# Queries of two cross-attention heads as one 2x2x2 block product in seven

## The chip, the cores and the metric

The kernel runs on one core of one Trainium2 chip. The metric is device microseconds (us) of one execution; a time is the median of several executions. Durations of single instructions and waits come from one further execution, which was taken with the hardware profiler.

## The reference

One layer of a streaming encoder on 512 tokens of width 1024, in float32:

```python
h = x + concat(A, B) @ W_out          # A: forgetting attention, B: gated recurrence
hn = rmsnorm(h, norm_x_g)
q = (hn @ w_q).reshape(b, s, 4, 256)  # 1024 x 1024 weights, four heads of 256 columns
k, v = split(rmsnorm(mem, norm_mem_g) @ w_kv)          # 256 memory tokens
p = softmax(q k^T / sqrt(256)); o = p v
h = h + o.reshape(b, s, 1024) @ w_o
h = h + square(relu(rmsnorm(h) @ w1)) @ w2             # d_ff = 4096
return rmsnorm(h)
```

The change concerns `hn @ w_q`, and in it heads 2 and 3: a product of 512 output columns, 512 tokens and an inner size of 1024.

## The kernel before

**Products.** Every float32 operand is kept as two tiles, `hi` (rounded to the matmul's type) and `lo` (what is missing), and each product is three matmuls: hi·hi, lo·hi and hi·lo (`gemm_fm`, L316 to L318). A weight panel of 1024 x 256 comes by DMA as two raw halves of 128 partitions x 1024 elements (`wr30a`, `wr30b`). Of each, ACT makes the hi part (L184, `wh...`), and DVE the lo part (L188, `wl...`). The split tiles live in four buffers, so the split of a panel half waits until the matmuls that read the half four places earlier are done. A panel's split is issued when an earlier panel is taken up by `next_panel`, and a scheduler gives it its place in the engine's order.

**Order.** Each engine runs its instructions in the order in which the program has them. A `fill` object holds generators of matmul groups (a "step" is the group for one or more slices of the inner size); `fill.run(x)` puts about x us of steps at this place of TensorE's order, and `fill.until(name)` all steps up to a named one.

**Cross attention.** After `residual(..., "wo", ...)`, which adds the output projection to the stream chunk by chunk (DVE L1317 `hT`, ACT L1318 `x1_hi`, DVE L1319 `x1_lo`), head 0's queries are projected (`x_proj(0)`), and the four heads then run one after the other. Per head and half of the tokens (`tp` 0 and 1): `x_scores` makes 12 matmuls of 256 columns (L1377 to L1379, `xs`), the row maximum on DVE (L1381, `xm`), its scaled negative (L1383, `xn`), two exponentials on ACT (L1388), a reciprocal (L1389) and two scalings on DVE (L1391, `xp`). `x_T_` transposes the probabilities on TensorE (L1400, `xpt`), ACT and DVE split them (L1451 `pth`, L1452 `ptl`), and `x_out` multiplies by the values (L1408 to L1410, `xo`) and writes `o_hi` (ACT, L1411) and `o_lo` (DVE, L1412). The scale of the softmax, `r16`, comes out of the mean square `pm1` by a short chain on GpSimd (L437, L440, L1368).

While a head's softmax runs on DVE and ACT, TensorE does filling work between the steps:

- in head 0, head 1's queries (`x_proj(1)`, tiles `xq10`, `xq11`);
- in heads 1 and 2, the queries of heads 2 and 3 (`x_proj(2)`, `x_proj(3)`: four tiles of 24 matmuls of 512 columns);
- in head 3, the first six of eight slices of three output chunks `xw0`, `xw1`, `xw2` of the next projection (`early` in `residual`); the rest follows `x_out(3)`.

**Sums of weights.** The feed-forward part that follows already uses products in seven. A weight sum for them is a copy of a block into DRAM (issued by SyncE, the list `copies`) and an accumulating DMA (issued by GpSimd, `Presum`), which are let go one by one at a pace given in us of TensorE work, `PACE`.

Of the kernel before, what the change touches and what calls it, by code (L numbers as in the profile page):

```python
# [39 lines left out]
SEVEN = (1, 2, 3, 4, 5, 6, 7)  # L40
RAWS, HB, LOADS = 5, 4, 8
COPIES = {12: 2, 19: 1, 20: 0, 24: 1}
PACE = (178.0, 4.7), (301.0, 11.5)


@with_exitstack
def emit(
# [49 lines left out]
    def s4(shape, name, dt=F32):  # L97
        return s4p.tile([P] + shape, dt, tag="s4", name=name)
# [7 lines left out]
    def t4(name):  # L106
        return t4p.tile([P, D], F32, tag="t4", name=name)
# [25 lines left out]
    def panel(w, n0):  # L133
        return [(slice(0, WT), w[:, n0 : n0 + WT].rearrange("(k p) n -> p k n", p=P))]
# [27 lines left out]
    LATE = len(specs)  # L162
    for j in range(4):
        specs.append(panel(w_xkv, j * WT))
    for w in (w_out, w_xq, w_xo):
        for j in range(4):
            specs.append(panel(w, j * WT))
    NG = DFF // HG
    stream = []
    state = {"used": 0, "halves": 0}  # L170
# [93 lines left out]
    def product_unit(name):  # L264
# [24 lines left out]
            jobs.append(lambda: load_block("5", "10", raw0["5"]))  # L289
        return jobs  # L290

    def next_panel():
        while len(stream) < min(state["used"] + 2, len(specs)):
# [95 lines left out]
    def run_now(gen):  # L389
        for _ in gen:  # L390
            pass
# [94 lines left out]
    def block2(g, rc):  # L486
        r, c = int(rc[0]), int(rc[1])
        k0 = g * HG + r * 2 * P
        return w2[k0 : k0 + 2 * P, c * S : (c + 1) * S].rearrange("(k p) n -> p k n", p=P)

    wsum = {}

    def sum_jobs(kind, g):
        block, shape = (block1, [P, UK, WT]) if kind == "u" else (block2, [P, 2, S])
        for name in SUMS:
            wsum[kind, g, name] = drp.tile(shape, F32, name=f"ws{kind}{g}{name}")

        def first(name):
            dma = nc.sync.dma_start(wsum[kind, g, name], block(g, SUMS[name][0]))
            copied.add((kind, g, name))  # L500
            return dma

        def sums():
            for name, (_, b) in SUMS.items():
                while (kind, g, name) not in copied:
                    copies.popleft()()
                src = wsum[kind, g, b] if b in SUMS else block(g, b)
                more = {"max_dma_last_dim": 2048} if b in SUMS else {}
                yield gp.dma_start(wsum[kind, g, name], src, accum_op=ALU.add, **more)  # L509

        return [lambda name=name: first(name) for name in SUMS], sums()
# [28 lines left out]
            return us  # L540

    presum = Presum()
    sets = []
# [4 lines left out]
    for i in range(0, len(sets), 2):  # L548
# [742 lines left out]
    def residual(src_hi, src_lo, g, dst_hi, dst_lo, name, ssq, order, nlast, after=None, hooks={}, open_end=False):  # L1291

        ps_, gens = {}, {}

        def open_(c):
            if c % 2 == 0:
                open_.wt = next_panel()
            ps_[c] = mm(f"{name}{c}")
            gens[c] = gemm_fm(ps_[c], open_.wt, (c % 2) * P, src_hi, src_lo, order=order)

        def early():

            for c in range(3):
                open_(c)
                for _ in range(KC - nlast):
                    yield next(gens[c])

        def rest():
            for c in range(KC):
                if c not in gens:  # L1310
                    open_(c)
                yield from gens[c]
                if open_end and c == KC - 1:
                    last_xw.append(ps_[c])
                    return
                hc = hTc(c)
                ve.tensor_tensor(hc, hc, ps_[c], ALU.add)  # L1317
                ac.activation(dst_hi[:, c, :], hc, AF.Identity, scale=g[:, c : c + 1])  # L1318
                ve.scalar_tensor_tensor(dst_lo[:, c, :], hc, g[:, c : c + 1], f(dst_hi[:, c, :]), op0=ALU.mult, op1=ALU.subtract)  # L1319
# [12 lines left out]

        return early, rest

    def mean_sq(ssq, name):
        pm = tr(name, (NT,))
        for tb in range(NT):
            te.matmul(pm[:, tb : tb + 1], ssq[:, tb * P : (tb + 1) * P], ones, start=True, stop=True)
        ms = sm(NT, name + "m")
        ve.tensor_scalar(ms, pm, 1.0 / D, None, op0=ALU.mult)  # L1340
        return ms
# [1 line left out]

    x1_hi, x1_lo = act_tile("x1_hi"), act_tile("x1_lo")
    ssq1 = t2("ssq1")
    _, wo_rest = residual(mx_hi, mx_lo, g_x, x1_hi, x1_lo, "wo", ssq1, (4, 5, 6, 7, 0, 1, 2, 3), 1)
    run_now(wo_rest())


    o_hi, o_lo = act_tile("o_hi"), act_tile("o_lo")  # L1350
    x2 = []
    xq, xps, xpr, xpT = {}, {}, {}, {}

    def x_proj(h):
        wt = next_panel()
        xq[h] = []
        for i in range(2):
            ps = mm(f"xq{h}{i}")
            yield from gemm_fm(ps, wt, i * P, x1_hi, x1_lo)
            a, b = q2(f"xqh{h}{i}"), q2(f"xql{h}{i}")  # L1360
            ac.activation(a, ps, AF.Copy)
            ve.tensor_tensor(b, ps, f(a), ALU.subtract)
            xq[h].append((a, b))

    run_now(x_proj(0))
    ms1 = mean_sq(ssq1, "pm1")
    r1 = rstd_of(ms1, NT, "r1")
    gp.tensor_scalar(r16, r1, 1.0 / 16.0, 0.0, op0=ALU.mult, op1=ALU.add)  # L1368

    def x_scores(h, tp):  # L1370
        ps = sc(f"xs{h}{tp}", (2, M))
        for j in range(2):
            ts_ = slice((2 * tp + j) * P, (2 * tp + j + 1) * P)
            for i in range(2):
                a, b = xq[h][i]
                kh_, kl_ = kTh[h][:, i, :], kTl[h][:, i, :]
                te.matmul(ps[:, j, :], a[:, ts_], kh_, start=i == 0, stop=False)  # L1377
                te.matmul(ps[:, j, :], a[:, ts_], kl_, start=False, stop=False)
                te.matmul(ps[:, j, :], b[:, ts_], kh_, start=False, stop=i == 1)  # L1379
        mx = sm(2, f"xm{h}{tp}")  # L1380
        ve.tensor_reduce(mx, ps, AX.X, ALU.max)  # L1381
        nm = sm(2, f"xn{h}{tp}")
        ve.scalar_tensor_tensor(nm, mx, -1.0, r16[:, 2 * tp : 2 * tp + 2], op0=ALU.mult, op1=ALU.mult)  # L1383
        den = sm(2, f"xd{h}{tp}")
        pr_ = t2(f"xp{h}{tp}", F32, (2, M))
        for j in range(2):
            tb = 2 * tp + j
            ac.activation(pr_[:, j, :], ps[:, j, :], AF.Exp, bias=nm[:, j : j + 1], scale=r16[:, tb : tb + 1], accum_out=den[:, j : j + 1])  # L1388
        ve.reciprocal(den, den)  # L1389
        for j in range(2):  # L1390
            ve.tensor_scalar(pr_[:, j, :], pr_[:, j, :], den[:, j : j + 1], None, op0=ALU.mult)  # L1391
        xpr[h, tp] = pr_
# [664 lines left out]
```

## Time and profile before

| | us |
|---|---|
| median of 3 executions | 748.14 (747.89 to 748.48) |
| the profiled execution, its own time | 748.24 |
| its span in the profile | 746.5 |
| TensorE busy | 738.6 (99% of the span) |
| DVE busy | 566.6 (76%) |
| ACT busy | 460.4 (62%) |
| GpSimd busy | 213.4 (29%) |
| granted TensorE clock, mean | 0.999 of full speed |

In rows of the profile, PE is TensorE's matmuls and PEld its weight loads, DVE is VectorE, ACT ScalarE, POOL GpSimd, SP SyncE; POOLq and SPq are their DMA queues. A row of the timeline gives the start in us, the duration in us, the engine, the line of the kernel, the operation, output<-inputs with buffer and tile numbers left out (`xq` is any of `xq00` to `xq31`), the size, and in brackets the idle time of the engine before it with what ended it.

### The profile page before, as it was taken

To read this page: it belongs to the slowest core of one execution; us is meant where nothing else is said; L and a number is where in the kernel's file an instruction comes from. 1 tells how busy PE (TensorE), PEld (TensorE's weight loads), DVE (VectorE), ACT (ScalarE), POOL (GpSimd) and SP (SyncE) were. 2 spreads that over 40 slices of the span, in tenths; PEclk is the share of its full clock that TensorE was granted. 3 is DMA by queue.
4 is the path that set the end of the run, shared out by engine and by line. 5 is a ranking of instruction groups with operands and counts; after the bars stand their busy time and mean duration, and the time that the engine had idled before them with its cause. 6 is when DMAs were issued, how large, how long until landed. Compare 5 with 4: busy or idle time off the path is not lost.

```text
span 746.5 us, 12316 instructions
## 1 busy us (share of the span) xinstructions
PE 738.6 (99%) x4557; PEld 645.3 (86%) x4557; DVE 566.6 (76%) x892; ACT 460.4 (62%) x769; POOL 213.4 (29%) x290
## 2 busy tenths in 40 slices
PE   9999999999999999999999999999999999999996
PEld 6889888898888888888888899898989898999985
DVE  5878997677787866655546898978787878878796
ACT  5875876666666733244435589666665757574864
POOL 7216842442342246621012111111111111100034
PEclk9999999999999999999999999999999999999999
DMA  7797999857955899976669799898989899978352
GB/s 245 217 245 199 259 306 315 279 169 229 336 170 186 274 221 195 213 151 133 125 155 209 117 241 233 243 247 220 241 220 236 209 246 227 234 192 247 120 112 114
DMA packets 111918, 159.22 MB, mean 213 GB/s; under 512 B 6337, under 2 KB 74218, under 8 KB 111858
## 3 DMA queue, kind: packets, MB, share of 16 engines
q1 hardware_dynamic: 85490, 114.62, 46.6%
q0 software_dynamic: 26208, 43.54, 33.0%
q8 instruction: 36, 0.59, 0.3%
q10 hardware_dynamic: 160, 0.27, 0.1%
q14 instruction: 24, 0.20, 0.1%
HBM read 153.15 MB, written 51.40 MB: 274 GB/s over the span
## 4 chain that ended last, share of the span: by engine, by line
PE 90%; DMA 3%; DVE 2%; ACT 2%; issue 1%; POOL 0%; POOLq 0%; DVEq 0%; SPq 0%; ACTq 0%
PE uU L1632 4%; PE uU L1634 4%; PE uU L1633 4%; PE U L1790 3%; PE U L1791 3%; PE U L1792 3%; PE uY L1634 2%; PE uY L1633 2%; PE uY L1632 2%; PE xk L1146 2%; PE xq L316 2%; PE wo L316 2%; PE xq L317 2%; PE xq L318 2%; PE xw L318 2%; PE xw L317 2%
## 5 line engine op out<-in xcount | busy, mean ns | idle before, releaser
L188 DVE TENSOR_TENSOR wlu<-wru,whu 128x1024 fp32r<-128x1024 f32 x53 | 63.9, 1219 | 25.9 <-ACT whu L184 25.9
L184 ACT ACTIVATE whu<-wru 128x1024 fp32r<-128x1024 f32 x53 | 55.9, 1059 | 40.7 <-PE U L1792 16.8
L188 DVE TENSOR_TENSOR wld<-wrd,whd 128x1024 fp32r<-128x1024 f32 x56 | 68.2, 1220 | 13.9 <-ACT whd L184 13.7
L184 ACT ACTIVATE whd<-wrd 128x1024 fp32r<-128x1024 f32 x56 | 59.0, 1054 | 15.3 <-PE uU L1633 6.6
L1790 PE MATMUL U<-whd,hb 128*128 128x512 f32 x120 | 46.8, 390 | 0.0
L1791 PE MATMUL U<-wld,hb 128*128 128x512 f32 x120 | 46.8, 390 | 0.0
L1792 PE MATMUL U<-whd,hb 128*128 128x512 f32 x120 | 46.7, 389 | 0.0
L509 POOL DMA_DIRECT2D wsd<-in_w_dram x16 | 17.8, 1114 | 68.2 <-PE xw L318 16.6
L1167 POOL TENSOR_SCALAR bi<-nF,Ft 128x128 f32<-128x128 f32 (+3 forms) x32 | 20.8, 659 | 56.2 <-PE pt L1203 30.4
L1632 PE MATMUL uU<-xs_hi,whu 128*128 128x256 f32 x128 | 36.3, 284 | 0.0
L1634 PE MATMUL uU<-x_hi,wlu 128*128 128x256 f32 x128 | 36.2, 283 | 0.0
L1632 PE MATMUL uY<-xs_hi,whu 128*128 128x256 f32 x128 | 36.2, 283 | 0.0
L1633 PE MATMUL uY<-xs_lo,whu 128*128 128x256 f32 x128 | 36.2, 283 | 0.0
L1634 PE MATMUL uY<-xs_hi,wlu 128*128 128x256 f32 x128 | 36.2, 283 | 0.0
L1634 PE MATMUL uU<-xs_hi,wlu 128*128 128x256 f32 x128 | 36.2, 283 | 0.0
L1633 PE MATMUL uU<-x_lo,whu 128*128 128x256 f32 x128 | 36.2, 283 | 0.0
L1633 PE MATMUL uU<-xs_lo,whu 128*128 128x256 f32 x128 | 36.2, 283 | 0.0
L1632 PE MATMUL uU<-x_hi,whu 128*128 128x256 f32 x128 | 36.2, 283 | 0.0
L1528 POOL DMA_DIRECT2D wrd<-in_w_dram x8 | 9.8, 1223 | 86.6 <-DVE wld L188 51.4
L509 POOL DMA_DIRECT2D wsu<-in_w_dram x14 | 17.0, 1211 | 44.3 <-PE xq L318 14.5
L1318 ACT ACTIVATE x_hi<-hT,gv 128x512 fp32r<-128x512 f32 x15 | 10.7, 714 | 25.8 <-DVE hT L1317 25.8
L1792 PEld LDWEIGHTS U<-whd,hb 128*128 128x128 f32 x120 | 22.5, 188 | 4.7
(1012 smaller groups left out, 2656.4 us busy)
## 6 DMA issues: line engine op xcount, KB each, us to landing
wru<-in_w_dram SPq DMA_DIRECT2D x25, 512.0 KB, 6.7
wsd<-in_w_dram SPq DMA_DIRECT2D x24, 512.0 KB, 6.9
wrd<-in_w_dram SPq DMA_DIRECT2D x24, 512.0 KB, 4.2
wrd<-wsd SPq DMA_DIRECT2D x24, 512.0 KB, 5.7
wsu<-in_w_dram SPq DMA_DIRECT2D x21, 512.0 KB, 7.2
wru<-wsu SPq DMA_DIRECT2D x21, 512.0 KB, 5.5
wsd<-in_w_dram POOLq DMA_DIRECT2D x16, 512.0 KB, 8.0
wsu<-in_w_dram POOLq DMA_DIRECT2D x14, 512.0 KB, 7.6
```

Of the source, the lines that this page charges most:

```text
L184: at = ac.activation(hi, raw, AF.Copy)
L188: at_lo = ve.tensor_tensor(lo, raw, f(hi), ALU.subtract)
L316: te.matmul(ps, wh, hi, start=n_ == 0 and not begun, stop=False)
L317: te.matmul(ps, wh, lo, start=False, stop=False)
L318: at = te.matmul(ps, wl, hi, start=False, stop=k == order[-1])
L509: yield gp.dma_start(wsum[kind, g, name], src, accum_op=ALU.add, **more)
L1632: te.matmul(ps[:, i, :], whi[:, k, ws], xh[:, k, :], start=begin, stop=False, skip_group_check=True)
L1633: te.matmul(ps[:, i, :], whi[:, k, ws], xl[:, k, :], start=False, stop=False, skip_group_check=True)
L1634: at = te.matmul(ps[:, i, :], wlo[:, k, ws], xh[:, k, :], start=False, stop=k == UK - 1, skip_group_check=True)
L1790: te.matmul(ps, hi, whi[:, k, :], start=begin, stop=False, skip_group_check=True)
L1791: te.matmul(ps, hi, wlo[:, k, :], start=False, stop=False, skip_group_check=True)
L1792: at = te.matmul(ps, lo, whi[:, k, :], start=False, stop=k == 1, skip_group_check=True)
```

## The change

Heads 0 and 1 keep `x_proj`. For heads 2 and 3 the product is cut into 2x2x2 blocks: inner size into two halves of 512, output columns into the two heads, and tokens into two halves of 256. Seven block products in place of eight give it, each of 4 slices x 2 column blocks x 3 matmuls = 24 matmuls of 256 columns. Each product has one left operand of 512 x 256 weights (block 00, 10, 11 or a DRAM-made sum for products 5, 6, 7; product 4 takes product 6's raw tile after block 10 was added to it by an accumulating DMA), and one right operand of token sums (`x1_sums`), which are put into `o_hi` and `o_lo` while these are unused. They run in the order 1, 2, 5, 6, 7, 4 and 3 and accumulate in three banks: U (products 1, 6, 7, 4), V (2, which begins with a copy of U on ACT, L1478) and Y (5 and 3; after product 6, U is copied into Y, L1497). Outputs: V is head 2's first token half, U after product 4 head 2's second, and Y+`y5` head 3 (DVE L1501 `xt`, with ACT L1466 and DVE L1468 or L1470 for the hi and lo parts).

Products 1, 2, 5, 6, 7, 4 are filling work of head 1, and product 3 and the first steps of `early` that of head 2. `early` now takes slices 0 to 3 of three chunks first, then 4 and 5. `next_panel` counts half panels, at most four ahead. GpSimd does the first part of the new weight sums, with `PACE` beginning at 164 in place of 178.

```diff
-PACE = (178.0, 4.7), (301.0, 11.5)
+PACE = (164.0, 4.7), (301.0, 11.5)
...
+    def x1_early():
+        dif.append(s4([UK, WT], "xdif"))
+        dif7.append(s4([UK, WT], "xdif7"))
+        for k in range(UK):
+            ac.activation(dif[0][:, k, :], hTc(k)[:, h2], AF.Identity, scale=g_x[:, k : k + 1])
+        for j in range(2):
+            ve.tensor_tensor(dif7[0][:, 2 * j : 2 * j + 2, :], hT[j][:, :, h1], hT[j][:, :, h2], ALU.subtract)
...
+        def step(c0, h, op):
+            for k in range(UK):
+                ve.scalar_tensor_tensor(d[:, k, :], hTc(c0 + k)[:, h], g_x[:, c0 + k : c0 + k + 1], d[:, k, :], op0=ALU.mult, op1=op)
+
+        def parts(name, sign):
+            hi, lo = x1s[name]
+            ac.activation(hi, d, AF.Copy, scale=sign)
+            if sign > 0:
+                ve.tensor_tensor(lo, d, f(hi), ALU.subtract)
+            else:
+                ve.scalar_tensor_tensor(lo, d, sign, f(hi), op0=ALU.mult, op1=ALU.subtract)
...
+        for k in range(UK):
+            ve.scalar_tensor_tensor(lo[:, k, :], d7[:, k, :], g_x[:, k : k + 1], f(hi[:, k, :]), op0=ALU.mult, op1=ALU.subtract)
+        step(UK, h2, ALU.subtract)
+        parts("5", 1.0)
+        step(0, h1, ALU.add)
+        parts("6", -1.0)
...
+    def q_product(g, name):
+        b = {"5": "Y", "3": "Y", "2": "V"}.get(name, "U")
+        if (g, b) not in qbank:
+            qbank[g, b] = mm(f"xq{b}{g}").rearrange("p (i n) -> p i n", i=2)
+            if b == "V":
+                ac.activation(qbank[g, b], qbank[g, "U"], AF.Copy)
+        ps = qbank[g, b]
+        (whi,), (wlo,) = next_panel()
+        xh, xl = x1s[name]
+        for k in range(UK):
+            for i in range(2):
...
+                te.matmul(ps[:, i, :], whi[:, k, ws], xh[:, k, :], start=begin, stop=False, skip_group_check=True)
+                te.matmul(ps[:, i, :], whi[:, k, ws], xl[:, k, :], start=False, stop=False, skip_group_check=True)
+                at = te.matmul(ps[:, i, :], wlo[:, k, ws], xh[:, k, :], start=False, stop=k == UK - 1, skip_group_check=True)
+            yield presum.tick(6 * WT / 2400, at)
...
+        elif name == "6":
+            ac.activation(qbank[g, "Y"], ps, AF.Copy)
+            x1_last()
+        elif name in "73":
+            t = t2(f"xt{name}{g}", F32, (2, M))
+            ve.tensor_tensor(t, ps, y5s[g], ALU.add)
+            q_out(2 * g + 1, 1 if name == "7" else 0, t, -1.0)
...
     for h in range(4):
-        if 0 < h < 3:
-            fill.add(x_proj(h + 1), f"xq{h + 1}")
-        elif h == 3:
+        if h == 1:
+            for g, name in QORDER[:-1]:
+                fill.add(q_product(g, name), f"q{g}{name}")
+        if h == 2:
+            fill.add(q_product(1, "3"), "q13")
...
             fill.add(early())
+        if h == 3:
+            fill.until("q13")
...
-        if h < 3:
-            fill.until(f"xq{h + 1}")
+        if h < 2:
+            fill.until(("xq1", "q14")[h])
```

DVE's order from the last chunk of the residual to head 0's first softmax, before (`hT` is the chunk's sum, `wl30b` to `wl31b` weight splits, `xql` the lo parts of head 0's queries):

```order
420 L1317 TENSOR_TENSOR hT_3304<-hT_3304,wo_3582 128x512
421 L188 TENSOR_TENSOR wl30b<-wr30b,wh30b 128x1024
422 L1319 SCALAR_TENSOR_TENSOR x_lo<-hT_3304,gv,x_hi 128x512
423 L1362 TENSOR_TENSOR xql_3655<-xq_3628,xqh_3654 128x512
424 L188 TENSOR_TENSOR wl31a<-wr31a,wh31a 128x1024
425 L1340 TENSOR_SCALAR pm1m<-pm_3688 128x4
426 L188 TENSOR_TENSOR wl31b<-wr31b,wh31b 128x1024
427 L1362 TENSOR_TENSOR xql_3685<-xq_3658,xqh_3684 128x512
428 L1381 TENSOR_REDUCE xm_3739<-xs_3726 128x2
```

The same place after (`xdif` is the sum of token blocks in the making, `o_lo` its lo parts, `wlq` the splits of the half panels of products 1 and 2):

```order
425 L1362 TENSOR_TENSOR hT_3310<-hT_3310,wo_3599 128x512
426 L1421 SCALAR_TENSOR_TENSOR xdif<-hT_3310,gv,xdif 128x256
427 L194 TENSOR_TENSOR wl30b<-wr30b,wh30b 128x1024
428 L1364 SCALAR_TENSOR_TENSOR x_lo<-hT_3310,gv,x_hi 128x512
429 L1435 SCALAR_TENSOR_TENSOR o_lo<-xdif_3470,gv,o_hi 128x256 x4
430 L1427 TENSOR_TENSOR o_lo<-xdif,o_hi 128x1024
431 L1421 SCALAR_TENSOR_TENSOR xdif<-hT_3304,gv,xdif 128x256
432 L1454 TENSOR_TENSOR xql_3672<-xq_3645,xqh_3671 128x512
433 L1421 SCALAR_TENSOR_TENSOR xdif<-hT_3304,gv,xdif 128x256
434 L1421 SCALAR_TENSOR_TENSOR xdif<-hT_3306,gv,xdif 128x256 x2
435 L194 TENSOR_TENSOR wlq_3738<-wrq_3739,whq_3737 128x1024
436 L1429 SCALAR_TENSOR_TENSOR o_lo<-xdif,o_hi 128x1024
```

Between chunk 7 and the first `xql` there are now seven more instructions, and four of the next five rows are new as well. Behind the last row follow `pm1m`, one `xdif`, the split of product 2's half panel, the second `xql`, three more `xdif`, and then head 0's `xm`.

ACT's order in head 1, before (`xp10` and `xp11` are the exponentials of the two token halves, `xqh20` the hi part of head 2's first query tile, `pth1` the transposed probabilities):

```order
316 L1388 ACTIVATE xp10_3873,xd10_3872<-xs10_3855,xn10_3870,r0_432 128x256 x2
317 L1388 ACTIVATE xp11_3919,xd11_3918<-xs11_3901,xn11_3916,r0_432 128x256 x2
318 L1361 ACTIVATE xqh20_3957<-xq20_3891 128x512
319 L1451 ACTIVATE pth1_3951<-xpt10_3941 128x512
320 L1451 ACTIVATE pth1_3951<-xpt11_3942 128x512
321 L184 ACTIVATE wh33a_4033<-wr33a_4035 128x1024
```

After (`whq17`, `whq14`, `whq13` are the splits of the half panels of products 7, 4, 3; `xqU1`, `xqV1`, `xqY1` the three banks; `wh38a` a split of the next projection's weights):

```order
324 L1528 ACTIVATE xp10_3910,xd10_3909<-xs10_3892,xn10_3907,r0_435 128x256 x2
325 L190 ACTIVATE whq17_3980<-wrq17_3982 128x1024
326 L1528 ACTIVATE xp11_3966,xd11_3965<-xs11_3948,xn11_3963,r0_435 128x256 x2
327 L1478 ACTIVATE xqV1_3978<-xqU1_3916 128x512
328 L190 ACTIVATE whq14_4032<-wrq16_3925 128x1024
329 L1466 ACTIVATE xqh20_4027<-xqV1_3978 128x512
330 L1595 ACTIVATE pth1_4021<-xpt10_4011 128x512
331 L1595 ACTIVATE pth1_4021<-xpt11_4012 128x512
332 L190 ACTIVATE whq13_4062<-wrq13_4064 128x1024
333 L1495 ACTIVATE xy51_4060<-xqY1_4031 128x512
334 L190 ACTIVATE wh38a_4130<-wr38a_4132 128x1024
335 L1497 ACTIVATE xqY1_4031<-xqU1_3916 128x512
```

Four splits of weights now stand among head 1's softmax and copies, one of them between the exponentials of the two halves, and two copies of a bank (rows 327 and 335) stand behind a split.

TensorE's order behind head 3's last value product `xo7`, before:

```order
1855 L1410 MATMUL xo7_4286<-pth3_4262,xvl1_2292 128x512
1856 L316 MATMUL xw1_4245<-o_hi_3614,wh33b_4037 128x512
1857 L317 MATMUL xw1_4245<-o_lo_3615,wh33b_4037 128x512
1858 L318 MATMUL xw1_4245<-o_hi_3614,wl33b_4038 128x512
1859 L316 MATMUL xw2_4311<-o_hi_3614,wh34a_4189 128x512
1860 L317 MATMUL xw2_4311<-o_lo_3615,wh34a_4189 128x512
```

After:

```order
1948 L1550 MATMUL xo7_4460<-pth3_4435,xvl1_2295 128x512
1949 L352 MATMUL xw0_4281<-o_hi_3631,wh38b_4134 128x512
1950 L353 MATMUL xw0_4281<-o_lo_3632,wh38b_4134 128x512
1951 L354 MATMUL xw0_4281<-o_hi_3631,wl38b_4135 128x512
1952 L352 MATMUL xw0_4281<-o_hi_3631,wh38b_4134 128x512
```

Before, the last slice of `xw1` and six slices of `xw2` (3 + 18 matmuls) stood between `xo7` and the slices that read the outputs of `xo6` and `xo7`; now `xw0`'s slices 6 and 7, which read them, follow at once.

More of the change, by code (lines that the diff above doesn't have):

```diff
@@ L164, in emit @@
         specs.append(panel(w_xkv, j * WT))
-    for w in (w_out, w_xq, w_xo):
-        for j in range(4):
-            specs.append(panel(w, j * WT))
+    for j in range(4):
+        specs.append(panel(w_out, j * WT))
+    for j in range(2):
+        specs.append(panel(w_xq, j * WT))
+    QORDER = [(1, name) for name in "1256743"]
+    QFIRST = len(specs)
+    specs += [lambda g=g, n=n: q_unit(g, n) for g, n in QORDER]
+    for j in range(4):
+        specs.append(panel(w_xo, j * WT))
     NG = DFF // HG
@@ L290, in product_unit, with parts_of, q_unit @@
         return jobs
+    def parts_of(i):
+        return 1 if QFIRST <= i < QFIRST + len(QORDER) else 2
+    q_raw = {}
+    def q_unit(g, name):
+        hi, lo = new_parts([UK, WT], f"q{g}{name}")
+        stream.append(([hi], [lo]))
+        if name == "4":
+            raw = q_raw.pop(g)
+        else:
+            if name == "6":
+                raw = q_raw[g] = s4([UK, WT], f"wrq{g}{name}")
+            else:
+                state["halves"] += 1
+                if state["halves"] % 3 == 0:
+                    raw = t4(f"wrq{g}{name}")
+                else:
+                    raw = wrp.tile([P, D], F32, tag="wr", name=f"wrq{g}{name}", padded_shape=[P, UK * UW])
+                raw = raw.rearrange("p (k n) -> p k n", k=UK)
+            if name in SUMS:
+                src = wsum["q", g, name]
+            else:
+                src = block_q(g, {"1": "00", "2": "10", "3": "11"}[name])
+            nc.sync.dma_start(raw, src)
+        jobs = [split_of(hi, lo, raw)]
+        if name == "6":
+            jobs.append(lambda: tc.keep_in_program_order(gp.dma_start(raw, block_q(g, "10"), accum_op=ALU.add)))
+        return jobs
     def next_panel():
-        while len(stream) < min(state["used"] + 2, len(specs)):
+        while len(stream) < len(specs) and sum(parts_of(i) for i in range(state["used"], len(stream) + 1)) <= 4:
             for split in load_next():
@@ L542, in emit @@
     presum = Presum()
-    sets = []
+    sets = [sum_jobs("q", 1)]
     for g in range(DFF // HG):
@@ L547, in emit @@
         sets.append(sum_jobs("d", g))
-    for i in range(0, len(sets), 2):
+    copies.extend(sets[0][0])
+    for i in range(1, len(sets), 2):
         for some in zip(*(c for c, _ in sets[i : i + 2])):
@@ L1301, in early @@
         def early():
[L1303 to L1306, printed above, removed]
+            for ks in (range(UK), range(UK, KC - nlast)):
+                for c in range(3):
+                    if c not in gens:
+                        open_(c)
+                    for _ in ks:
+                        yield next(gens[c])
         def rest():
@@ L1345, in emit @@
     ssq1 = t2("ssq1")
-    _, wo_rest = residual(mx_hi, mx_lo, g_x, x1_hi, x1_lo, "wo", ssq1, (4, 5, 6, 7, 0, 1, 2, 3), 1)
+    dif, dif7 = [], []
+    def x1_early():
[3 more added lines that the diff above has]
+            ac.activation(dif[0][:, k, :], hTc(k)[:, h2], AF.Identity, scale=g_x[:, k : k + 1])
+        for j in range(2):
+            ve.tensor_tensor(dif7[0][:, 2 * j : 2 * j + 2, :], hT[j][:, :, h1], hT[j][:, :, h2], ALU.subtract)
+    _, wo_rest = residual(mx_hi, mx_lo, g_x, x1_hi, x1_lo, "wo", ssq1, (4, 5, 6, 7, 0, 1, 2, 3), 1, hooks={3: x1_early})
     run_now(wo_rest())
@@ L1351, in emit, with x1_sums, last @@
     x2 = []
-    xq, xps, xpr, xpT = {}, {}, {}, {}
+    xq, xps, xpr, xpT = {h: {} for h in range(4)}, {}, {}, {}
+    x1s = {"1": (x1_hi[:, 0:UK, h1], x1_lo[:, 0:UK, h1])}
+    for name, h in (("2", h1), ("4", h2)):
+        x1s[name] = x1_hi[:, UK:KC, h], x1_lo[:, UK:KC, h]
+    def x1_sums():
+        halves_ = [t.rearrange("p k (h n) -> p (k h) n", h=2) for t in (o_hi, o_lo)]
+        for i, name in ((1, "5"), (2, "6"), (2, "3"), (3, "7")):
+            x1s[name] = tuple(t[:, UK * i : UK * i + UK, :] for t in halves_)
+        d, d7 = dif[0], dif7[0]
+        def step(c0, h, op):
[6 more added lines that the diff above has]
+                ve.tensor_tensor(lo, d, f(hi), ALU.subtract)
+            else:
+                ve.scalar_tensor_tensor(lo, d, sign, f(hi), op0=ALU.mult, op1=ALU.subtract)
+        hi, lo = x1s["7"]
+        for k in range(UK):
+            ac.activation(hi[:, k, :], d7[:, k, :], AF.Identity, scale=g_x[:, k : k + 1])
+        for k in range(UK):
[4 more added lines that the diff above has]
+        parts("6", -1.0)
+        def last():
+            step(UK, h1, ALU.subtract)
+            parts("3", -1.0)
+        return last
     def x_proj(h):
         wt = next_panel()
-        xq[h] = []
         for i in range(2):
@@ L1362, in x_proj, with q_out, half @@
             ve.tensor_tensor(b, ps, f(a), ALU.subtract)
-            xq[h].append((a, b))
+            for tp in range(2):
+                xq[h].setdefault(tp, []).append(tuple(t[:, tp * M : tp * M + M] for t in (a, b)))
+    qbank, y5s = {}, {}
+    def q_out(h, tp, src, sign):
+        def half(part):
+            name = f"xq{part}{h}{tp}"
+            return q2(name).rearrange("p (i n) -> p i n", i=2) if h % 2 == 0 else t2(name, R, (2, M))
+        a, b = half("h"), half("l")
+        ac.activation(a, src, AF.Copy, scale=sign)
+        if sign > 0:
+            ve.tensor_tensor(b, src, f(a), ALU.subtract)
+        else:
+            ve.scalar_tensor_tensor(b, src, sign, f(a), op0=ALU.mult, op1=ALU.subtract)
+        xq[h][tp] = [(a[:, i, :], b[:, i, :]) for i in range(2)]
+    def q_product(g, name):
[7 more added lines that the diff above has]
+        xh, xl = x1s[name]
+        for k in range(UK):
+            for i in range(2):
+                ws, begin = slice(i * P, (i + 1) * P), name in "15" and k == 0 and i == 0
+                te.matmul(ps[:, i, :], whi[:, k, ws], xh[:, k, :], start=begin, stop=False, skip_group_check=True)
+                te.matmul(ps[:, i, :], whi[:, k, ws], xl[:, k, :], start=False, stop=False, skip_group_check=True)
+                at = te.matmul(ps[:, i, :], wlo[:, k, ws], xh[:, k, :], start=False, stop=k == UK - 1, skip_group_check=True)
+            yield presum.tick(6 * WT / 2400, at)
+        if name == "2":
+            q_out(2 * g, 0, ps, 1.0)
+        elif name == "4":
+            q_out(2 * g, 1, ps, 1.0)
+        elif name == "5":
+            y5s[g] = t2(f"xy5{g}", F32, (2, M))
+            ac.activation(y5s[g], ps, AF.Copy)
+        elif name == "6":
[5 more added lines that the diff above has]
+            q_out(2 * g + 1, 1 if name == "7" else 0, t, -1.0)
     run_now(x_proj(0))
+    x1_last = x1_sums()
     ms1 = mean_sq(ssq1, "pm1")
@@ L1372, in x_scores @@
         for j in range(2):
-            ts_ = slice((2 * tp + j) * P, (2 * tp + j + 1) * P)
+            ts_ = slice(j * P, (j + 1) * P)
             for i in range(2):
-                a, b = xq[h][i]
+                a, b = (t[:, ts_] for t in xq[h][tp][i])
                 kh_, kl_ = kTh[h][:, i, :], kTl[h][:, i, :]
-                te.matmul(ps[:, j, :], a[:, ts_], kh_, start=i == 0, stop=False)
-                te.matmul(ps[:, j, :], a[:, ts_], kl_, start=False, stop=False)
-                te.matmul(ps[:, j, :], b[:, ts_], kh_, start=False, stop=i == 1)
+                te.matmul(ps[:, j, :], a, kh_, start=i == 0, stop=False)
+                te.matmul(ps[:, j, :], a, kl_, start=False, stop=False)
+                te.matmul(ps[:, j, :], b, kh_, start=False, stop=i == 1)
         mx = sm(2, f"xm{h}{tp}")
```

7 lines of the change are left out of this document (6 added, 1 removed).

## The prediction

> **What bounds the kernel now.** I read the page first (busy times and the chain that ended last), then the waits of TensorE, then the windows of the stage around the change.
>
> ```profile
> PE 738.6 (99%) x4557; PEld 645.3 (86%) x4557; DVE 566.6 (76%) x892; ACT 460.4 (62%) x769; POOL 213.4 (29%) x290
> ...
> PE 90%; DMA 3%; DVE 2%; ACT 2%; issue 1%; POOL 0%; POOLq 0%; DVEq 0%; SPq 0%; ACTq 0%
> ```
>
> ```profile
> PE warm L428 <- DVE ones L432: 1.3, 1, 1.3
> PE dg L867 <- ACT fv L793: 0.4, 1, 0.4
> ```
>
> ```profile
> 308.50:323.10 14.60, 14.60 (x70) 12.08 (x68) 8.34 (x8) 4.85 (x6) 7.32 (x7) 1.00 1.03 219
> 323.10:375.00 51.90, 51.90 (x281) 44.82 (x280) 29.45 (x55) 23.44 (x48) 7.32 (x8) 1.00 0.65 135
> 375.00:425.00 50.00, 50.00 (x243) 41.93 (x243) 30.55 (x53) 22.99 (x45) 9.67 (x10) 1.00 0.78 155
> ```
>
> TensorE carries the span, and it waits for nothing in the cross attention: its only two waits, 1.3 and 0.4 us, lie elsewhere, and in the windows (columns: length, then busy time of PE, PEld, DVE, ACT, POOL, then clock, DMA share, GB/s) it is busy for the whole of each at clock 1.00. So any matmul time taken away is a gain in full, and any wait put in is a loss in full. Nothing behind the stage can give time back, because TensorE does not wait there either. The sum is thus TensorE's work saved, less its new waits. It is made against the profiled execution, 748.24 us (span 746.5 and 1.74 outside it), 0.1 above the median of 748.14. About 0.2%, 1.5 us, is what a measurement of this kernel can tell.
>
> **TensorE's work.** The spacing of starts counts, not the duration shown.
>
> ```profile
> 347.76 0.39 PE L316 MATMUL xq<-x_hi,wh31a 128*128 128x512 f32 x1
> ...
> 352.53 0.39 PE L1408 MATMUL xo<-pth,xvh 128*128 128x512 f32 x1
> ```
>
> ```profile
> 438.15 0.28 PE L1634 MATMUL uU<-xs_hi,wlu 128*128 128x256 f32 x1
> ...
> 440.67 0.28 PE L1634 MATMUL uU<-xs_hi,wlu 128*128 128x256 f32 x1
> ```
>
> 21 matmuls of 512 columns lie in the 4.77 us of the first pair, 0.227 each; 21 of 256 columns in the 2.52 us of the second, 0.120 each. Removed are 4 x 24 of the first kind, 21.8 us; added are 7 x 24 = 168 of the second, 20.2 us. **Saved: 1.6 us.** Half the columns cost 0.53 of the time, so an eighth less arithmetic is only 7% less time, and this is the most that the change can win.
>
> [...]
>
> **New waits.** A product that begins from a bank's copy, or takes up a bank being copied, makes TensorE wait for ACT, whose order decides.
>
> ```profile
> 342.64 0.28 PE L1379 MATMUL xs<-kT,xql 128*128 128x256 f32 x1
> 342.76 0.40 PE L316 MATMUL xq<-x_hi,wh31a 128*128 128x512 f32 x1
> 342.96 0.69 DVE L1381 TENSOR_REDUCE xm<-xs 128x2 f32<-128x512 f32 x1 [0.47 <-PE xs L1379]
> 343.94 0.56 ACT L1388 ACTIVATE xp<-xs,xn,r 128x256 f32<-128x256 f32 x1 [2.30 <-DVE xn L1383]
> 344.50 0.56 ACT L1388 ACTIVATE xp<-xs,xn,r 128x256 f32<-128x256 f32 x1
> 344.94 0.20 ACT L1388 ACTIVATION_READ_ACCUMULATOR xp<-xs,xn,r 128x1 f32 x1
> 345.17 0.17 DVE L1389 RECIPROCAL xd<-xd 128x2 f32<-128x2 f32 x1 [1.33 <-ACT xp L1388]
> ```
>
> ```profile
> 450.03 0.58 ACT L1642 ACTIVATE uV<-uU 128x512 f32<-128x512 f32 x1
> 455.45 0.58 ACT L1647 ACTIVATE uY<-uU 128x512 f32<-128x512 f32 x1 [0.26 <-PE uU L1634]
> ```
>
> ```profile
> L188 DVE TENSOR_TENSOR wlu<-wru,whu 128x1024 fp32r<-128x1024 f32 x53 | 63.9, 1219 | 25.9 <-ACT whu L184 25.9
> L184 ACT ACTIVATE whu<-wru 128x1024 fp32r<-128x1024 f32 x53 | 55.9, 1059 | 40.7 <-PE U L1792 16.8
> ```
>
> A reader starts 0.32 after the last matmul's start (342.64 to 342.96), two exponentials with their sums take 343.94 to 345.14, 1.20 in all, a copy of a bank 0.58, a split 1.06 on ACT and 1.22 on DVE. For a handover I take 0.1.
>
> *Product 2.* Let T be the start of product 1's last step, right behind head 1's second scores (342.76 in the rows of before). Its six matmuls end the row at T+0.72; the reader of the last can start at T+0.60+0.32 = T+0.92. In ACT's order the split `whq17` comes next; its buffer is the one product 1 reads, so it runs T+0.92 to 1.98. Only then come the exponentials of the second half (ready at 343.94, T+1.18), to T+3.18, then the copy U to V, to T+3.76, and product 2 starts at about T+3.86 in place of T+0.72: **3.15 us**. Were the split out of the way, the exponentials would still end at T+2.38 and the wait be 2.35; I keep 2.3 to 4.0 for the range.
>
> *Product 7* writes U while Y is copied from it after product 6. Ahead of the copy stands the split `wh38a`, which waits for product 6's own end: 0.20 + 1.06 + 0.58 + 0.1 = **1.95 us** (0.9 with the split done earlier). *Product 4* overwrites nothing that ACT copies, but it adds to U, which DVE reads for `xt71` after product 7: 0.20 + 0.69 (the size of `xm` above) + 0.1 = **1.0 us**. Product 5 begins a bank without a copy, and 6 follows on it with V read by others: no wait. Product 4's raw tile needs an accumulating DMA before its split:
>
> ```profile
> wru<-in_w_dram POOLq DMA_DIRECT2D x7, 512.0 KB, 10.7
> ```
>
> Issued behind the split of product 6 at about 339, it lands at about 350 by this median, and the split `whq14` can run from product 2's end, by the walk above 350.7. Being late by up to 4 us costs nothing, since TensorE has products 5 and 6 (5.8 us) first.
>
> *Head 0.* DVE now makes token sums between the last chunk of the residual and head 0's first maximum: 13 of 128x256 and two of 128x1024.
>
> ```profile
> 308.70 0.69 DVE L1317 TENSOR_TENSOR hT<-hT,wo 128x512 f32<-128x512 f32 x1 [0.58 <-PE wo L318]
> 309.57 2.08 DVE L188 TENSOR_TENSOR wl30b<-wr30b,wh30b 128x1024 fp32r<-128x1024 f32 x1 [0.18 <-ACT wh30b L184]
> 311.58 1.78 DVE L1319 SCALAR_TENSOR_TENSOR x_lo<-hT,gv,x_hi 128x512 fp32r<-128x512 f32 x1
> 314.81 0.69 DVE L1362 TENSOR_TENSOR xql<-xq,xqh 128x512 fp32r<-128x512 f32 x1 [1.45 <-ACT xqh L1361]
> 320.41 0.16 DVE L1340 TENSOR_SCALAR pm1m<-pm 128x4 f32<-128x4 f32 x1 [1.36 <-PE pm L1338]
> 324.73 0.69 DVE L1381 TENSOR_REDUCE xm<-xs 128x2 f32<-128x512 f32 x1 [2.37 <-PE xs L1379]
> 330.17 0.81 DVE L1391 TENSOR_SCALAR xp<-xp,xd 128x256 f32<-128x256 f32 x2
> ```
>
> ```profile
> L1860 DVE SCALAR_TENSOR_TENSOR fo<-acc,fr,gfin x1: 485/485/485, 742.0 to 742.0; 128x256 f32<-128x256 f32 x1
> ...
> L1708 DVE SCALAR_TENSOR_TENSOR xs_lo<-xd,xs_hi x1: 1224/1224/1224, 432.8 to 432.8; 128x1024 fp32r<-128x1024 f32 x1
> ```
>
> 13 x 0.48 + 2 x 1.22 = 8.7 us. DVE's free time there is 14.60 - 8.34 = 6.3 in the window to 323.10 and 1.6 more to 324.73, 7.9 together: it does not fit. Walking the order of after through these durations, the second `xql` ends at 324.3 and the first maximum starts at 325.8 in place of 324.73.
>
> ```profile
> 323.69 0.28 PE L1379 MATMUL xs<-kT,xql 128*128 128x256 f32 x1
> ...
> 330.79 1.04 PE L1400 MATMUL xpt<-ident,xp 128*128 128x128 f32 x8
> ```
>
> The sixth matmul of the scores, at 323.69, needs that `xql`: 0.7. The last scaling, which ended at 330.98, ends at about 332.2; TensorE, 0.7 late, reaches the second four transposes at 330.79 + 0.4 + 0.7 = 331.9 (half of the eight are taken from 330.79 to 331.58): 0.4 more. **Together 1.1 us**, 0.3 to 2.5, since the stretched rows 2.08 and 1.78 show that DVE can run at nearly half pace here. GpSimd's chain:
>
> ```profile
> 320.67 1.15 POOL L437 TENSOR_SCALAR r1e<-pm1m 128x4 f32<-128x4 f32 x1 [3.98 <-DVE pm1m L1340]
> ...
> 323.04 0.20 POOL L1368 TENSOR_SCALAR r<-r 128x4 f32<-128x4 f32 x1
> 323.57 0.97 POOL L509 DMA_DIRECT2D wsd<-wsd  x1 [0.33 <-issue]
> ```
>
> It took 2.6 us from `pm1m`'s end; `pm1m` moves to about 322.0, and an issue of 1 us now stands in the chain: 325.7, just ahead of the 326.5 at which `xn` needs it. No term, but part of that range.
>
> *Head 2.* Let T2 be the start of product 3's last step, behind the second scores. ACT: `wh39b` (its buffer is product 3's) T2+0.92 to 1.98, exponentials to 3.18, `xqh30` to 3.76. DVE's order puts `xql30` (0.69) ahead of the last scaling (0.81): 4.45, then 5.26, and 0.1. TensorE has 0.72 of product 3, 12 matmuls of `xw0` (2.72) and four transposes (0.4): T2+3.84. **1.5 us**, 0.6 without the split.
>
> *After the last head*, TensorE loses its cover:
>
> ```profile
> 355.45 0.60 ACT L1411 ACTIVATE o_hi<-xo 128x512 fp32r<-128x512 f32 x1 [0.76 <-PE xo L1410]
> ```
>
> From an `xo`'s last matmul it takes 0.43 to ACT's start (352.53 + 11 x 0.227 = 355.02), then 0.60 and 0.69 on DVE and a handover: 1.8 us to `o_lo`. Before, 21 matmuls (4.8 us) hid this; now the reader is the fifth matmul behind, 5 x 0.227 = 1.1 later: **0.7 us**. Head 3's transposes and `x_out(2)` come with slack by the same walk, and the extra 1.5 MB of copies start where the DMA share is below 0.8, so both stand at nothing.
>
> **Sum:** -1.6 + 3.15 + 1.95 + 1.0 + 1.1 + 1.5 + 0.7 = +7.8, and 756.0 us. With the low ends -1.6 + 2.3 + 0.9 + 0.9 + 0.3 + 0.6 + 0.5 = +3.9, 752.1; with the high ends (4.0, 2.2, 1.2, 2.5, 2.0, 0.9) +11.2, 759.4.
>
> **The rivals.** *The splits do not hold the copies* (buffers free earlier than I read): the low ends, about 752.4. The row "whu<-wru" above speaks against it, with 16.8 us of ACT's idle time before splits ended by TensorE. 0.05.
>
> *The clock falls.* Product 2's wait is over 3 us, and the first row of TensorE in the trace shows what an unready array costs:
>
> ```profile
> 1.29 3.17 PE L428 MATMUL warm<-zero 128*128 128x512 bf16 x7 [1.29 <-DVE ones L432]
> ```
>
> Seven in 3.17 us are 0.45 each, twice 0.227. If the 24 matmuls of product 2 ran so, at 0.24, 2.9 us would come on top: 758.9. Against it: 3.15 is a short stop, and the exponentials may be earlier. 0.07. [...]
>
> *Only bare turn-arounds wait*, the one that ends on the other side, not slower. In the feed-forward part ACT reaches the copy 0.26 after the product. If it does so here, the two copies cost 0.2 + 0.58 + 0.1, 0.9 each, `xt71` 0.7 and the rest hides: -1.6 + 2.5 = +0.9, 749.1. It decides if all waits stay under 3.1 us. Against it: head 1's exponentials stand ahead of the first copy and start only 0.3 behind its product. 0.04. *All waits covered*, 746.6: 0.04, as a bound for what the order view may hide.
>
> *A late DMA.* DMA share is 1.03 in 308.50 to 323.10, where the raw halves of the first products are loaded. A load 3 us late gives 759. 0.05. That the change does not do what it says is ruled out by the order: 168 matmuls stand in place of 96.
>
> **How the numbers follow.** 0.75 for the forecast, 756.0. The range 751.5 to 760 takes in its bounds and the clock and DMA cases and leaves out the last two and tails. Faster by over 0.2%: 0.04; within: 0.04; slower: 0.92.
>
> **What would show it.** In the profile after: TensorE's waits view lists the first matmul of product 2 behind ACT's L1478 with some 3 us, product 7 behind L1497 with 2, product 4 behind DVE's L1501 with 1, transposes (L1540) behind L1531 in heads 0 and 2, and `xw0` behind L1552. Wrong I am if `xqV` starts without a wait, or if the waits sum to less than 3 us.

## The result, and the profile after

| | before | after |
|---|---|---|
| median, us | 748.20 (747.89 to 749.27, 6 executions) | 755.35 (753.82 to 755.91, 6 executions) |
| profiled execution, us | 748.24 | 755.39 |
| its span, us | 746.5 | 753.6 |

The ratio is 1.009, with a 95% interval of 1.0077 to 1.0103: 7.1 us slower, where 7.8 were forecast and the range was 3.3 to 11.8. The page after, TensorE's busy time and the chain that ended last:

```profile
PE 740.1 (98%) x4629; PEld 648.6 (86%) x4629; DVE 584.5 (78%) x918; ACT 470.8 (62%) x786; POOL 219.1 (29%) x294
...
PE 88%; DMA 4%; DVE 4%; issue 2%; ACT 2%; POOL 0%; POOLq 0%; DVEq 0%; ACTq 0%; SPq 0%
```

TensorE's share of the chain falls from 90 to 88%. Its waits after (engine, line it waited at, what released it, total, times, longest):

```profile
PE xqV L1485 <- ACT xqV L1478: 2.6, 1, 2.6
PE xqU L1485 <- ACT xqY L1497: 1.5, 1, 1.5
...
PE xqU L1485 <- DVE xt L1501: 0.8, 1, 0.8
PE pk L1098 <- ACT A L1061: 0.5, 1, 0.5
PE xpt L1540 <- DVE xp L1531: 0.4, 1, 0.4
PE lv L982 <- ACT mix L958: 0.4, 1, 0.4
PE xw L353 <- DVE o_lo L1552: 0.2, 1, 0.2
```

All five waits in the cross attention are ones that the forecast had named, with the releasers it had named; head 0's transposes, which it had named too, do not wait. (`pk` and `lv` lie far ahead of the change; `pk` waits between nothing and 1.8 us in the profiles of this study, so it is scatter of an execution.) A wait here counts from the modelled end of the last matmul; against the spacing of starts each costs about 0.16 to 0.25 more. They sum to 6.5 us so. Less the 1.6 us saved, that would make the kernel 4.9 us slower, and it is 7.1. The rest is seen in the timeline of TensorE around product 2:

```profile
343.84 0.28 PE L1487 MATMUL xqU<-x_hi,wlq 128*128 128x256 f32 x1
346.73 0.47 PE L1485 MATMUL xqV<-x_hi,whq 128*128 128x256 f32 x1 [2.61 <-ACT xqV L1478]
347.00 0.42 PE L1486 MATMUL xqV<-x_lo,whq 128*128 128x256 f32 x1
347.21 0.41 PE L1487 MATMUL xqV<-x_hi,wlq 128*128 128x256 f32 x1
...
349.99 0.41 PE L1485 MATMUL xqV<-x_hi,whq 128*128 128x256 f32 x1
350.20 0.34 PE L1486 MATMUL xqV<-x_lo,whq 128*128 128x256 f32 x1
350.37 0.28 PE L1487 MATMUL xqV<-x_hi,wlq 128*128 128x256 f32 x1
350.49 0.28 PE L1485 MATMUL xqV<-x_hi,whq 128*128 128x256 f32 x1
...
351.20 1.03 PE L1540 MATMUL xpt<-ident,xp 128*128 128x128 f32 x8
```

Behind the stop, starts are 0.213 us apart in place of 0.120, until 350.2; the 24 matmuls take 4.47 us in place of 2.88, **1.6 us lost**. The windows name it: in the second row the granted clock (the column behind the busy times) is 0.53.

```profile
343.20:346.70 3.50, 0.92 (x8) 0.72 (x6) 2.38 (x5) 2.64 (x6) 0.00 (x0) 1.00 0.97 154
346.70:350.20 3.50, 3.47 (x16) 3.47 (x17) 0.38 (x2) 0.00 (x0) 0.00 (x0) 0.53 0.45 152
```

Finally head 0's queries, 48 matmuls, in TensorE's timeline of before, from their first start to the mean square's:

```profile
308.50 0.39 PE L316 MATMUL xq<-x_hi,wh29a 128*128 128x512 f32 x1
...
319.43 0.39 PE L1338 MATMUL pm<-ones,ssq 128*128 128x1 f32 x3
```

The same two rows after:

```profile
308.63 0.39 PE L352 MATMUL xq<-x_hi,wh29a 128*128 128x512 f32 x1
...
319.81 0.39 PE L1383 MATMUL pm<-ones,ssq 128*128 128x1 f32 x3
```

10.93 us became 11.18: 0.25 lost, ahead of the place where the forecast put head 0's loss.

The stage from the first of these starts to the first matmul of the feed-forward part (`uU`, at 425.46 us before and 432.86 us after) took 116.96 us before and 124.23 us after, 7.27 us more. It is used again below, because the part ahead of it scatters: in the ten profiles its first start lies anywhere from 307.8 to 311.6 us.

### The profile page after: what moved, and what is told of

Same layout as the page of the kernel before. It is cut to its first block, busy times and chain, and to the rows that moved or that the text cites. A ratio compares the mean times of both kernels' runs of the same rounds, so it can differ in the third digit from the quotient of the medians.

```text
span 753.6 us, 12520 instructions
## 1 busy us (share of the span) xinstructions
PE 740.1 (98%) x4629; PEld 648.6 (86%) x4629; DVE 584.5 (78%) x918; ACT 470.8 (62%) x786; POOL 219.1 (29%) x294
## 4 chain that ended last, share of the span: by engine, by line
PE 88%; DMA 4%; DVE 4%; issue 2%; ACT 2%; POOL 0%; POOLq 0%; DVEq 0%; ACTq 0%; SPq 0%
PE uU L1776 4%; PE uU L1778 4%; PE uU L1777 4%; PE U L1934 4%; PE U L1935 4%; PE U L1936 4%; PE uY L1778 2%; PE uY L1777 2%; PE uY L1776 2%; PE xk L1189 2%; PE wo L352 2%; PE wo L354 2%; PE Y L1934 2%; PE Y L1936 2%; PE Y L1935 2%; PE wo L353 2%
## 5 line engine op out<-in xcount | busy, mean ns | idle before, releaser
L1672 POOL DMA_DIRECT2D wru<-in_w_dram x7 | 9.2, 1320 | 80.0 <-DVE wlu L194 80.0
```

The lines of the kernel that those rows point to most:

```text
L1672: tc.keep_in_program_order(gp.dma_start(box[0], block(g, "10"), accum_op=ALU.add))
```

## The experiments

The theory: the change saves 1.6 us of matmuls and pays for it with stops, each a loss by itself, and the longest stop also costs clock. Its rivals: product 2 is slow for another reason than the stop; or the stops only stand where some other bound (late sums, DVE) would hold TensorE anyway, and come back elsewhere when removed.

**The clock.** Matmuls that do nothing useful go into the stop ahead of product 2: 18, 6 and 3 of them.

```diff
+        elif name == "1":
+            warm_ = pvt("xwarm")
+            for _ in range(18):
+                te.matmul(warm_[:, 0:WT], kTh[0][:, 0, 0:P], x1_hi[:, 0, h1], start=True, stop=True)
```

> The changed kernel with 18 matmuls of 256 columns more, into a spare bank whose content nobody reads, between product 1 and product 2, where TensorE stands still for 2.9 us. If it is the stop that halves the clock, product 2 follows a stop of about 0.6 us, runs at 0.12 us a matmul in place of 0.19, and 24 matmuls win 1.6 us: 753.7 us, although there is more work. If product 2 is slow for another reason (its bank, its operands), nothing is won: 755.4 us.

Measured 753.76 us (753.03 to 754.46), 1.0073 of before (1.0058 to 1.0088): 1.6 us below the changed kernel with more work in it. The two intervals overlap, so the time alone does not show the gain; the trace does. The stage takes 122.75 us in place of 124.23. The timeline of TensorE with 18:

```profile
343.15 2.32 PE L1496 MATMUL xwarm<-x_hi,kT 128*128 128x256 f32 x18
345.92 0.39 PE L1485 MATMUL xqV<-x_hi,whq 128*128 128x256 f32 x1 [0.45 <-ACT xqV L1478]
346.14 0.28 PE L1486 MATMUL xqV<-x_lo,whq 128*128 128x256 f32 x1
346.26 0.28 PE L1487 MATMUL xqV<-x_hi,wlq 128*128 128x256 f32 x1
...
348.89 1.04 PE L1544 MATMUL xpt<-ident,xp 128*128 128x128 f32 x8
```

The copy still ends the wait, but product 2 takes 2.97 us, with starts 0.12 apart behind the first. Bank and operands are the same as in the changed kernel: the stop made it slow.

> The same with only 6 extra matmuls, which leave a stop of about 1.9 us. The changed kernel's stop of 1.5 us (product 7) left the clock alone and that of 2.6 us (product 2) did not; this one lies between. Clock kept: 753.7 us; clock lost: 755.4 us. [...]

> The changed kernel with 3 extra matmuls before product 2, which leave a stop of about 2.25 us, between the 1.9 us behind which the profiled product 2 ran at full pace and the 2.6 us behind which it ran at half the clock for 3.5 us. Clock kept: product 2 takes 2.9 us and the time is about 753.8 us; clock lost: product 2 takes 4.5 us and the time is about 755.4 us.

With 6 the median was 754.64 us (753.64 to 756.64), with 3 it was 754.95 (753.05 to 756.26): between the two forecasts. Product 2's first start in TensorE's timeline with 6:

```profile
346.52 0.39 PE L1485 MATMUL xqV<-x_hi,whq 128*128 128x256 f32 x1 [1.89 <-ACT xqV L1478]
```

Its first starts with 3, and the one at which the spacing falls back to 0.12:

```profile
346.95 0.39 PE L1485 MATMUL xqV<-x_hi,whq 128*128 128x256 f32 x1 [2.25 <-ACT xqV L1478]
347.17 0.29 PE L1486 MATMUL xqV<-x_lo,whq 128*128 128x256 f32 x1
347.29 0.38 PE L1487 MATMUL xqV<-x_hi,wlq 128*128 128x256 f32 x1
347.47 0.41 PE L1485 MATMUL xqV<-x_hi,whq 128*128 128x256 f32 x1
...
350.67 0.31 PE L1485 MATMUL xqV<-x_hi,whq 128*128 128x256 f32 x1
```

In the profiled executions the clock survived a stop of 1.89 us and not one of 2.25. There it fell only 0.4 us after the restart and came back 3.4 us later.

By the traces it is not the length of the stop alone that decides, but also where it lies. In the profile after, the record of the granted clock starts at 5.56 us, and the clock changes at 346.89, 350.30 and 753.07 us: the slow stretch lasts 3.413 us, and those at full clock ahead of it and behind it 341.33 and 402.77 us, 100 and 118 times as long. With 3 extra matmuls it changes at 347.32, 350.73 and 750.09 us, 1 and 117 such steps apart. In the other eight profiles the one fall within the span lies 216 to 218 whole steps behind the start of the clock's record (before: 737.28 us, from 7.03 to 744.31). The last fall of each profile, at 742 to 753 us, comes 2.0 to 5.1 us after the last matmul, where TensorE stands still until the end. TensorE's idle time in single steps (by the modelled ends of matmuls), and the clock in the step that follows:

| step, us | profile | TensorE idle in it, us | clock in the next step |
|---|---|---|---|
| 343.47 to 346.89 | after, stop ahead of product 2 | 2.61 | half |
| 343.90 to 347.32 | 3 extra matmuls, the same stop | 2.25 | half |
| 746.68 to 750.09 | 3 extra matmuls, behind the last matmul | 1.97 | half |
| 746.25 to 749.66 | after, behind the last matmul | 1.70 | full |
| 357.13 to 360.54 | after, stop ahead of product 7 | 1.52 | full |
| 342.70 to 346.11 | 6 extra matmuls, first part of the stop of 1.89 | 1.48 | full |

In all ten profiles, within the span, each step with 1.97 us or more of idle time was followed by half the clock, and none with 1.70 us or less. The stop of 1.89 us was cut in two by the end of a step, 1.48 and 0.41 us, so the profile does not tell whether 1.89 us inside one step would have cost clock. Where the steps lie against the program differs from one execution to the next (the record starts at 7.03 us before and at 5.56 us after), which fits the scatter: of the four executions with 6 extra matmuls two had a mean clock of 0.998 (753.64 and 754.28 us) and two 0.996 (754.99 and 756.64); of the changed kernel's six, the two fastest (753.82, 754.58) had 0.998 and 0.999, the others 0.995 to 0.997. With 18, all four had 0.999. Half the clock for 3.5 us is 0.0023 of the mean, about the difference. But the fall behind the last matmul takes up to 0.0025 off the mean as well, and single executions of the kernel before had 0.996 and 0.997, so the mean alone does not prove a slow product 2 in an execution without a profile.

**The two copies.** V is copied right behind product 1, and the order of the products is changed so that another product stands between a copy and its reader.

```diff
-    QORDER = [(1, name) for name in "1256743"]
+    QORDER = [(1, name) for name in "1526743"]
...
-            if b == "V":
-                ac.activation(qbank[g, b], qbank[g, "U"], AF.Copy)
...
+        elif name == "1":
+            qbank[g, "V"] = mm(f"xqV{g}").rearrange("p (i n) -> p i n", i=2)
+            ac.activation(qbank[g, "V"], ps, AF.Copy)
```

> Products in the order 1, 5, 2, 6, 7, 4, 3, with V copied from U right behind product 1, so that product 5 (24 x 0.12 = 2.9 us) runs during the copy. If the stop before product 2 and the slow clock behind it cost what the trace shows (2.8 + 0.15 + 1.6), the time falls by 4.5 us to 750.8 us, with the waits before products 7 and 4 left as they are. If the time is bound by something else there (late sums, DVE), it stays above 753.5 us.

Measured 751.19 us (750.13 to 754.01, 8 executions), 1.0042 of before (1.0029 to 1.0055). The waits at `xqV` are gone and those behind it stand as they were:

```profile
PE xqU L1483 <- ACT xqY L1498: 1.5, 1, 1.5
...
PE xqU L1483 <- DVE xt L1502: 0.8, 1, 0.8
```

The second step puts product 2 behind product 6, where Y is copied: the order string is `"1562743"`.

> Products in the order 1, 5, 6, 2, 7, 4, 3, V copied behind product 1 and Y behind product 6, so that product 2 hides the second copy too. The sum of waits falls by another 1.7 us: 749.1 us, with product 4's wait for DVE (0.9 us) left. Rival: product 6 now overwrites U while V is copied, and takes over the wait: 750.8 us or more.

Measured 749.28 us (748.57 to 750.23, 10 executions), 1.0014 of before (1.0005 to 1.0023). Of the waits on a copy none is left, and product 6 did not take one over: its predecessor 5 covers V's copy. The medians fell by 4.2 and 1.9 us, where 4.5 and 1.7 were expected. The first of these compares two series of executions, in which the kernel before took 748.20 and 748.50 us; the stage in the traces is free of that: 124.23, then 119.89, then 118.13 us, that is 4.3 and 1.8 us less. So both steps gave back what their stops had cost, and nothing else held TensorE there.

**The other waits.** First the move of head 1's `x_out`:

```diff
-            fill.until(("xq1", "q14")[h])
+            fill.until(("xq1", "q17")[h])
...
         x_out(h, pth, ptl)
+        if h == 1:
+            fill.until("q14")
```

> Products in the order 1, 5, 6, 2, 7, 4, 3 as before, and head 1's x_out, 12 matmuls of 2.7 us, moved between product 7 and product 4, so that DVE's xt71 (0.7) is done under it. If product 4's wait of 0.94 us is a real loss, it goes and nothing replaces it: 0.9 us less than without the move, 748.3 us. Rival: scores of head 2 now follow product 4 at once and wait for its outputs, so nothing is won.

Measured 748.06 us (746.35 to 748.42), 0.9994 of before (0.9985 to 1.0004): level with it. The wait on `xt` is off the list, and two of those in the cross attention are left:

```profile
PE xpt L1541 <- DVE xp L1532: 0.5, 1, 0.5
...
PE xw L353 <- DVE o_lo L1553: 0.2, 1, 0.2
```

Then these two as well. Products 4 and 3 both go between head 2's two scores (the `fill.until("q14")` behind `x_out` goes again), so that the splits which wait for them are done before the second exponentials; and after the last head, slice 6 of all three chunks goes ahead of slice 7.

```diff
         x_scores(h, 0)
         fill.run(X1)
+        if h == 2:
+            fill.until("q13")
...
         def rest():
+            if open_end:
+                for c in range(3):
+                    yield next(gens[c])
```

> All waits covered: order 1, 5, 6, 2, 7, 4, 3; head 1's x_out behind product 7; products 4 and 3 both between the two scores of head 2, so that no split stands between the exponentials; and after the last head slice 6 of the three chunks ahead of slice 7. With every stop gone only TensorE's work is left, 1.6 us less than before: 146.9 + 600, that is 746.9 us, 0.998 of before. If a wait takes a new place (head 2's softmax late behind 5.8 us of products, its fill used up early), it stays at 748 us or above.

Measured 747.34 us (746.26 to 748.92, 11 executions), 0.9988 of before (0.9977 to 0.9998). Both waits went, and one came:

```profile
PE xo L1553 <- DVE ptl L1602: 0.2, 1, 0.2
```

By starts it is 0.5 us: head 2 had taken up so much filling work that only 3 matmuls stood between head 3's transposes and its `x_out`. The last kernel moves one step of it:

```diff
-        fill.run(X2 + X3)
+        fill.run(X2 + X3 - (0.7 if h == 2 else 0.0))
```

> As the kernel with all waits covered, but one step (3 matmuls, 0.7 us) of the filling work behind head 2's second scores is moved on to head 3, where x_out waited 0.5 us for DVE's ptl with only 3 matmuls between it and the transposes; now there are 6. Expected: that wait goes, 746.8 us, 0.998 of before. Rival: head 2's second softmax now comes too late for its transposes, and the 0.5 us moves there: 747.3 us.

Measured 747.06 us (746.60 to 748.69, 11 executions), 0.9988 of before (0.9979 to 0.9996). The rival came true in the trace: `xo`'s wait went and head 2's transposes wait again, 0.5 us by starts.

```profile
PE xpt L1544 <- DVE xp L1535: 0.3, 1, 0.3
```

The sum closes within the scatter: -1.6 for the matmuls, +0.25 in head 0's queries and +0.5 for the one wait make -0.85 us. The stage took 116.31 us with all waits covered and 116.25 us in the last kernel, 0.65 and 0.71 us less than before, and 0.12% of 748.3 is 0.9. The intervals of both kernels exclude no change only barely.

## Why the prediction was right, point by point

The sign and the mechanism of the stops held: every stop but head 0's was where the forecast had put it, and taking them away one by one gave the time back. That the size was met so closely is partly luck. The terms, by the spacing of starts:

| term | forecast, us | measured, us |
|---|---|---|
| matmuls saved | -1.6 | -1.6 (product 1's first 18 start 0.120 apart) |
| head 0, token sums on DVE | +1.1 | +0.25, at another place |
| product 2 waits for V | +3.15 | +2.8 |
| clock behind it | 0 (a rival, +2.9 at 0.07) | +1.6 |
| product 7 waits for Y | +1.95 | +1.7 |
| product 4 waits for `xt` | +1.0 | +0.9 |
| head 2's transposes | +1.5 | +0.65 |
| `xw0` waits for `o_lo` | +0.7 | +0.5 |
| sum | +7.8 | +6.8 (the stage from 308.6 to the feed-forward's first matmul grew by 7.3) |

The 0.5 us between the sum and the stage are single matmuls around the stops that start about 0.1 us late each. So the total was met by two errors of opposite sign. **The waits were all too long**, by 2.6 us together, and **the clock was wrongly ruled unlikely**.

The first error is one step: the walks through DVE's and ACT's order added durations, while TensorE was counted by the spacing of starts. ACT's chain ahead of product 2 in the profile after:

```profile
344.04 1.06 ACT L190 ACTIVATE whq<-wrq 128x1024 fp32r<-128x1024 f32 x1 [2.01 <-PE xqU L1486]
345.01 0.55 ACT L1528 ACTIVATE xp<-xs,xn,r 128x256 f32<-128x256 f32 x1
345.46 0.19 ACT L1528 ACTIVATION_READ_ACCUMULATOR xp<-xs,xn,r 128x1 f32 x1
345.55 0.55 ACT L1528 ACTIVATE xp<-xs,xn,r 128x256 f32<-128x256 f32 x1
346.00 0.20 ACT L1528 ACTIVATION_READ_ACCUMULATOR xp<-xs,xn,r 128x1 f32 x1
346.09 0.59 ACT L1478 ACTIVATE xqV<-xqU 128x512 f32<-128x512 f32 x1
```

Each instruction starts 0.09 to 0.11 us before the one ahead of it ends: the split takes 0.97 of the chain and not 1.06, the exponentials 1.08 and not 1.20. The split also began 0.80 us after product 1's last step and not 0.92, since it waits for the last matmul that reads the hi part (L1486), not for the last of the product. From the copy's end (346.68) to product 2's first start (346.73) it is 0.05 us, where the walk had an estimate of 0.1. On DVE the effect is as large:

```profile
309.55 0.48 DVE L1421 SCALAR_TENSOR_TENSOR xdif<-hT,gv,xdif 128x256 f32<-128x256 f32 x1
309.95 2.06 DVE L194 TENSOR_TENSOR wl30b<-wr30b,wh30b 128x1024 fp32r<-128x1024 f32 x1
...
313.65 1.66 DVE L1435 SCALAR_TENSOR_TENSOR o_lo<-xdif,gv,o_hi 128x256 fp32r<-128x256 f32 x4
315.23 1.21 DVE L1427 TENSOR_TENSOR o_lo<-xdif,o_hi 128x1024 fp32r<-128x1024 f32 x1
...
325.12 0.69 DVE L1521 TENSOR_REDUCE xm<-xs 128x2 f32<-128x512 f32 x1 [0.57 <-PE xs L1519]
```

Four sums of 0.48 take 1.58 us to the next start, 0.40 each, so 13 cost 5.1 and not 6.3 us. The forecast said that DVE's work "does not fit"; it fitted, with 0.57 us idle before head 0's first maximum, which waited for TensorE as before. What was lost there, 0.25 us, came earlier: one new sum stands ahead of the last chunk's split and `x_lo`, which TensorE reads in head 0's queries. In head 2 the same overlap counts, and the first two of the second four transposes need only the first of the two scalings.

The second error is the rival "the clock falls". The forecast held 3.15 us to be "a short stop"; the stop was even shorter, 2.6 us, and the clock halved. Its price was 1.6 and not 2.9 us, because the slow phase lasted 3.5 us, in which 16 of the 24 matmuls ran. That a stop of 3.15 us is a short one is shown by no run; a stop of 2.25 us was enough with 3 extra matmuls, where it lay inside one step of 3.413 us. The other rivals did not occur: the splits did hold the copies, TensorE waited for more than bare turn-arounds, and the accumulating DMA was not on the list of waits.

## What to carry to other kernels

On an engine that never waits, price a rewrite by the spacing of starts: an eighth less arithmetic in half-width matmuls was 7% less time, 1.6 us, and one bank copy behind a full ACT queue cost more than that. Read the order of the engine that does the copy, ask what in front of it waits for the same product, and put another product between a copy and its reader; with the copies and the other waits covered the same arithmetic went from 7.1 us slower to 0.9 us faster. In such walks use start-to-start times for every engine (here 0.40 us in place of 0.48 for DVE's sums, 0.97 in place of 1.06 for ACT's split), and count a TensorE stop of about 2 us or more as one that may cost clock on top (2.25 us did in one profile, 1.89 us did not in another). An estimate from the steps above: a single stop under 1.7 us would cost none, one over 3.9 us (twice 1.97) would cost clock, and between them it would depend on where the steps lie.

## What the runs showed of the hardware that was not expected

A TensorE stop of 2.25 to 2.6 us was followed by 3.4 to 3.5 us at about half the clock (0.53 granted; starts of 256 columns 0.213 us apart in place of 0.120). The clock did not fall at a fixed time after TensorE's work ended (3.8 us behind the last matmul before, 5.1 us after, 1.97 us with 3 extra matmuls), but at the end of a step of 3.413 us, and the steps ran on through the execution (after, the first change lies 100 steps behind the start of the clock's record, and the third 118 behind the second). A step with 1.97 us of idle time was followed by half the clock, one with 1.70 us was not.
